# Two layers of four parallel mixers: half of the pool and conv denses moved ahead of the attention, five filler matmuls a step

## The chip, the cores and the metric

The kernel runs on one core of one Trainium2 chip. The metric is the device time of one execution in microseconds (us), here the median of three runs. TensorE (PE in the profile) does matmuls, VectorE (DVE) and ScalarE (ACT) the elementwise work, GpSimd (POOL) a few small operations and some DMAs, and SyncE (SP) issues most DMAs. Each engine takes its own instructions in the order in which the compiler left them and waits on semaphores for the others.

## The reference: what is computed

Two layers of a decoder trunk over 512 tokens of width 1024, all in float32:

```
h = rmsnorm(x, norm_g);  proj = h @ w_in           # split into the inputs of everything below
o_nsa  = nsa_mixer(...)    # compressed + selected + window attention, 4 heads of 64
o_pool = pool_mixer(...)   # causal means over 2, 4, 8, 16 tokens, then a 64x64 mix per group
o_conv = conv_mixer(...)   # b * (3-tap causal convolution of c * x)
o_fox  = fox_mixer(...)    # attention with forgetting gates, 4 heads of 64
branch_i = (o_i * silu(gates_i)) @ w_branch[i]     # 256 -> 1024
acc = sum_i sigmoid(merge_i) * branch_i            # merge_i: 4 x 1024 columns of proj
x = x + acc @ w_out                                # a final rmsnorm after the second layer
```

## The kernel before

Activations lie transposed: 128 features on the partitions, 512 tokens along the free dimension. Every float32 operand is split into a high part, rounded to the matmul's input format, and a low part, the rest (`split`, lines 69 to 76: ScalarE copies the high part, VectorE subtracts), and a product is three matmuls: high by high, high by low, low by high. A *dense* (lines 288 to 310) makes 128 output features for all tokens: 8 blocks of the 1024 inputs times 3 products, 24 matmuls of 512 columns into one of three PSUM banks `ps_d`. Its weights come by one 512 KB DMA into `wr`, and are split into `wh` and `wl`, two buffers each. Its result is taken over by a generator (`evac`) that is pumped one step for every second matmul, so that its VectorE and ScalarE steps fall under the next dense.

A layer runs in this order. The inputs of the compressed keys, of the selection and window keys and of the queries, then the values (`v_group`). Then eight gate denses, with the compressor's small products between them. Then the attention: 12 units, two for each of four NSA heads and one for each of four forgetting heads. A unit has four score products (`S`, lines 643 to 667: two matmuls into `ps_s`, a fused add and minimum on VectorE, the exponential with its sum on ScalarE, a reciprocal and a normalisation on VectorE), three groups of transposes (`T`, lines 673 to 681, 3 + 4 + 3 blocks into `ps_pt`, which are then split into `ptx`), and three groups of four matmuls with the values (`PV`, lines 683 to 703, into `ps_o`). After a head's last PV, `head_out` adds the two halves, multiplies by the gate and splits the result into `y`.

A loop over 57 steps (lines 1200 to 1216) lays the units out, one score product a step, the transposes from four steps later, the PV from seven. After each step it takes `FILL` matmuls from a chain of denses, the *filler* (lines 1170 to 1183): 4 denses for the forgetting heads, 4 for the first half of pool and convolution, 4 for the second half, 6 merge logits, 18 x 24 = 432 matmuls in all, of which 48 are taken before the loop. That is only the order in which the program is written. A scheduler puts each engine's instructions in an order of its own by what it takes to be ready, so that filler and merge denses can stand earlier than they are written.

After the attention come the branch products (`branches`, lines 821 to 844, 24 matmuls for each of four blocks of output features), the first of which are scheduled among the last attention steps; the rest of the merge logits; a second half of the merge with seven products in place of eight (`merge`); and the output projection. Its last block also gives the sum of squares for the next norm: `add_square` (line 238) squares a block of 128 features on ScalarE and adds it on VectorE to the blocks before it; `sum_squares` (line 229) then sums over the partitions with four one-column matmuls by a vector of ones. It does so once for the first seven blocks, when the seventh is added, and once for the eighth.

At the start, `ng` (norm gains, 128 x 24) is loaded on GpSimd's queue (line 1054). Each block of x is multiplied by it as it is split (`x_parts`). 16 idle matmuls on ones (line 1073) run before the first dense.

Of the kernel before, what the change touches and what calls it, by code (L numbers as in the profile page):

```python
# [16 lines left out]
T = 512  # L17
# [4 lines left out]
MERGE0 = 52  # L22
FILL = 7
ACT_NORM = ()
# [20 lines left out]
def trunk_kernel(ctx: ExitStack, tc: tile.TileContext, xT, w_all, par_all, const, gains, rope, outT):  # L45
# [47 lines left out]
    class Stream:  # L93
# [60 lines left out]
        def load(self, slot="wr"):  # L154
            i = self.loaded
            self.loaded += 1
            c = self.cols(i)
            self.slots.pop(next(n for n, x in enumerate(self.slots) if x is slot))
            if slot == "wr":
                t = sb([128, 1024], "wr", 3)  # L160
            elif slot == "rope":
                t = sb([128, 2, T], "rope", 1).rearrange("p a b -> p (a b)")
            else:
                t = slot
            l, j = self.order[i]
            if i == 0:
                for n in range(2):
                    nc.scalar.dma_start(t[:, n * 512:n * 512 + 512], w_all[l, j, :, n * 512:n * 512 + 512])
            else:
                nc.sync.dma_start(t[:, :c], w_all[l, j, :, :c])  # L170
            self.raw[i] = t, slot
# [65 lines left out]

    def add_square(src, m, bias=0.0, sq=None):
        n = src.shape[-1]
        sq = (temp() if sq is None else sq)[:, :n]  # L240
        ACT.activation(sq, src, AF.Square, bias=bias)
        if m in (0, 7):
            state["sq"] = sq
        else:
# [4 lines left out]
            else:  # L249
                DVE.tensor_tensor(state["sq"], state["sq"], sq, ALU.add)  # L250
            if m == 6:
                sum_squares(n, True, False)

    def stats(n=T, keep=False):
        sum_squares(n, False, True)
        p = state["ssq"]
# [796 lines left out]

    nc.gpsimd.dma_start(ng, gains)
    xr = []
# [16 lines left out]
    idle = psum("s", 2)  # L1072
    for n in range(16):
        PE.matmul(idle[:, 128:T], tri_ones[:, 128:256], tri_ones[:, 128:T], start=n == 0, stop=n == 15)

# [18 lines left out]
    for l in range(L):  # L1094
# [43 lines left out]
        def ev_gate(i, f):  # L1138
# [7 lines left out]
            return g  # L1146

        ch = None
        for n, (i, f) in enumerate(GATES):
# [5 lines left out]
            if n == 3:  # L1155
                drain()
                ch = itertools.chain(cmp_k(), cmp_v())
        drain()
        run(ch)
# [10 lines left out]
        def filler():  # L1170
            for f in range(2):
                yield from dense(rhs, ev_fq)
                yield from dense(rhs, ev_fk)
            yield from dense(rhs, ev_pool(0))
            yield from dense(rhs, ev_conv("x", 0))
            yield from with_mix(dense(rhs, ev_conv("c", 0)))
            yield from dense(rhs, ev_conv("b", 0))
            yield from dense(rhs, ev_pool(1))
# [3 lines left out]
            for m, i in LOGITS[:4 + AHEAD]:  # L1182
                yield from dense(rhs, ev_merge(m, i))

        def with_mix(d):
            for n, _ in enumerate(d):
                if n == 3:
                    mx = pool_mix()
                    next(mx)
                    bg.append(mx)  # L1190
                yield

# [56 lines left out]
        else:  # L1249
            xn = []  # L1250

            def ev_last(m, c):
                def g(acc):
# [3 lines left out]
                    DVE.tensor_tensor(x, acc[:, :c.stop - c.start], x, ALU.add)  # L1257
                    add_square(x, m)
                    if m == 1:
# [29 lines left out]
    for half in range(2):  # L1289
# [3 lines left out]
        drain()  # L1293
        _, rb = stats(T // 2, keep=True)
        x = xn[KT - 1][:, c]
# [56 lines left out]
def _layout(np, a):  # L1352
# [8 lines left out]
    for l in range(L):  # L1361
# [12 lines left out]
        for n, (i, h) in enumerate(GATES):  # L1374
            tiles.append(feat(run(2448 + 256 * i + 128 * h)))
            if n < 4:
                tiles.append(hid(n // 2, n % 2))
        for h in range(2):
            tiles += [feat(run(1676 + 128 * h)), feat(run(1932 + 128 * h))]
        for h in range(2):  # L1380
            tiles += [feat(run(s + 128 * h)) for s in (652, 908, 1420, 1164)]
        pairs = lambda m: [m[256 * j:256 * j + 256].reshape(2, 128, 512).transpose(1, 0, 2).reshape(128, 1024)
# [52 lines left out]
```

## Time and profile before

| | us |
|---|---|
| median of three runs | 954.16 (953.74 to 955.42) |
| the profiled execution | 953.55 |
| its span, first to last instruction | 951.0 |
| PE busy | 936.2 (98%) |
| VectorE busy | 714.0 (75%) |
| ScalarE busy | 520.0 (55%) |
| mean granted TensorE clock | 0.997 of full speed |

Busy time is the sum over stages with different limits, so the share of a stage says more than that of the span. A matmul's reported length is longer than the distance to the next one, as matmuls overlap: the pace is read from a run of them. A chain of waits follows the work that ended last backwards, at each step to what released it.

### The profile page before, as it was taken

The page shows a single profiled execution, that of the slowest core. Times are in us where ns is not written, and L with a number is a line of the kernel's source. Part 1 is how long each engine was busy: PE and PEld are TensorE (multiplying, and loading weights), DVE is VectorE, ACT ScalarE, POOL GpSimd, SP SyncE. Part 2 cuts the span into 40 slices and gives each one's busy share as a digit, 9 for nine tenths or more (in the row PEclk, how much of TensorE's full clock was granted, in tenths as well). Part 3 has the DMA queues.
Part 4 walks back from the last instruction along what each step waited for, and adds up shares of the span by engine and source line. Part 5 has one row for each costly group of instructions (what it writes and reads, how often), then busy time and mean ns, then how long its engine had stood idle before and what let it go on. Part 6 is the DMA issues. An engine that isn't in the chain of part 4 may idle for free.

```text
span 951.0 us, 12852 instructions
## 1 busy us (share of the span) xinstructions
PE 936.2 (98%) x4696; PEld 795.4 (84%) x4696; DVE 714.0 (75%) x1392; ACT 520.0 (55%) x906; POOL 31.1 (3%) x45
## 2 busy tenths in 40 slices
PE   9999999999999999999999999999999999999996
PEld 7988888888878888887889888888888788888796
DVE  6694689986787977776668548999677878686765
ACT  7295475575545554544426636656665455546273
POOL 0000000000000000000100000000000000010002
PEclk9999999999999999999999999999999999999998
DMA  7253222222236667643515421221322557686353
GB/s 268 80 175 113 74 83 68 78 89 89 67 122 173 171 207 213 177 155 134 189 63 170 135 89 67 89 67 45 111 67 79 177 159 201 200 210 194 112 168 121
DMA packets 39614, 124.73 MB, mean 131 GB/s; under 512 B 4464, under 2 KB 6528, under 8 KB 39552
## 3 DMA queue, kind: packets, MB, share of 16 engines
q1 hardware_dynamic: 35712, 112.38, 36.0%
q0 software_dynamic: 2976, 10.50, 5.5%
q10 hardware_dynamic: 864, 1.05, 0.3%
q8 instruction: 36, 0.59, 0.3%
q14 instruction: 26, 0.21, 0.1%
HBM read 119.72 MB, written 4.19 MB: 130 GB/s over the span
## 4 chain that ended last, share of the span: by engine, by line
PE 95%; DVE 2%; ACT 1%; DMA 1%; issue 1%; POOL 0%; DVEq 0%; SPq 0%; ACTq 0%; POOLq 0%
PE ps_d L303 56%; PE ps_d L988 9%; PE ps_s L988 5%; PE ps_o L698 3%; PE ps_pt L676 3%; PE ps_pt L988 2%; PE ps_pt L1026 2%; PE ps_s L554 2%; PE ps_pt L554 2%; PE ps_s L832 2%; PE ps_s L653 2%; PE ps_s L652 1%; PE ps_pt L832 1%; PE ps_o L1026 1%; PE ps_d L1026 1%; PE ps_o L415 1%
## 5 line engine op out<-in xcount | busy, mean ns | idle before, releaser
L303 PE MATMUL ps_d<-xh,wh 128*128 128x512 f32 x632 | 248.9, 394 | 1.9 <-ACT wh L72 1.9
L303 PE MATMUL ps_d<-xl,wh 128*128 128x512 f32 x632 | 248.6, 394 | 0.5 <-DVE xl L76 0.5
L72 ACT ACTIVATE wh<-wr 128x1024 fp32r<-128x1024 f32 (+2 forms) x134 | 139.0, 1038 | 153.9 <-PE ps_d L303 70.1
L73 DVE TENSOR_TENSOR wl<-wr,wh 128x1024 fp32r<-128x1024 f32 (+2 forms) x134 | 160.3, 1199 | 52.5 <-ACT wh L72 50.8
L303 PE MATMUL ps_d<-xh,wl 128*128 128x512 f32 x632 | 174.0, 392 | 0.0
L303 PEld LDWEIGHTS ps_d<-xh,wh 128*128 128x128 f32 x632 | 118.9, 188 | 25.7 <-ACT wh L72 3.0
L303 PEld LDWEIGHTS ps_d<-xl,wh 128*128 128x128 f32 x632 | 118.8, 188 | 24.0 <-DVE xl L76 1.5
L303 PEld LDWEIGHTS ps_d<-xh,wl 128*128 128x128 f32 x632 | 117.5, 188 | 23.1
L657 ACT ACTIVATE p<-p,nm 128x128 f32<-128x128 f32 (+1 forms) x96 | 53.3, 556 | 35.1 <-DVE nm L655 34.8
L324 DVE TENSOR_TENSOR t<-ps_d,rstd 128x512 f32<-128x512 f32 x74 | 50.7, 685 | 26.7 <-PE ps_d L303 26.3
L655 DVE CUSTOM_DVE_ANT_0 p<-ps_s,cst 128x128 f32<-128x128 f32 (+1 forms) x96 | 45.6, 484 | 13.0 <-PE ps_s L653 6.8
L72 ACT ACTIVATE ptx<-ps_pt 128x384 fp32r<-128x384 f32 (+1 forms) x72 | 36.9, 521 | 23.1 <-PE ps_o L698 14.3
L698 PE MATMUL ps_o<-ptx,V 128*128 128x256 f32 (+1 forms) x288 | 48.8, 282 | 0.6 <-DVE ptx L73 0.6
L698 PEld LDWEIGHTS ps_o<-ptx,V 128*128 128x128 f32 x288 | 42.4, 190 | 3.6 <-DVE ptx L73 0.8
L73 DVE TENSOR_TENSOR ptx<-ps_pt,ptx 128x384 fp32r<-128x384 f32 (+1 forms) x72 | 42.0, 592 | 2.1 <-ACT ptx L72 2.0
L676 PE MATMUL ps_pt<-cst,p 128*128 128x128 f32 x240 | 40.1, 276 | 0.0
L303 PE MATMUL ps_d<-y,wh 128*128 128x256 f32 (+1 forms) x176 | 38.0, 336 | 0.9 <-ACT y L75 0.9
L303 PE MATMUL ps_d<-st,wh 128*128 128x256 f32 (+1 forms) x176 | 33.5, 332 | 0.0
L73 DVE TENSOR_TENSOR wl<-V,wh 128x1024 fp32r<-128x1024 f32 x18 | 22.0, 1222 | 13.1 <-ACT wh L72 13.1
L303 PEld LDWEIGHTS ps_d<-y,wh 128*128 128x128 f32 x176 | 27.9, 190 | 4.2 <-ACT y L75 1.4
L72 ACT ACTIVATE wh<-V 128x1024 fp32r<-128x1024 f32 x18 | 19.1, 1062 | 21.9 <-PE ps_s L832 6.5
L676 PEld LDWEIGHTS ps_pt<-cst,p 128*128 128x128 f32 x240 | 28.1, 140 | 3.3
(343 smaller groups left out, 1736.4 us busy)
## 6 DMA issues: line engine op xcount, KB each, us to landing
wr<-in_w_all_dram SPq DMA_DIRECT2D x143, 512.0 KB, 3.3
V<-in_w_all_dram SPq DMA_DIRECT2D x26, 512.0 KB, 3.5
rope<-in_w_all_dram SPq DMA_DIRECT2D x12, 512.0 KB, 4.6
t<-in_xT_dram SPq DMA_DIRECT2D x16, 256.0 KB, 4.6
V<-in_w_all_dram POOLq DMA_DIRECT2D x8, 512.0 KB, 8.2
wr<-in_w_all_dram SPq DMA_DIRECT2D x8, 400.0 KB, 3.1
wr<-in_w_all_dram POOLq DMA_DIRECT2D x6, 512.0 KB, 6.8
ptc<-in_xT_dram SPq DMA_DIRECT2D x8, 256.0 KB, 3.1
```

The lines of the kernel that those rows point to most:

```text
L72: ACT.activation(hi, src, AF.Copy)
L73: DVE.tensor_tensor(lo, src, f32(hi), ALU.subtract)
L303: PE.matmul(acc[:, :width], w, r[k][:, tok], start=(n == 0), stop=(n == 23))
L324: DVE.tensor_tensor(t, acc, state["rb"], ALU.mult)
L554: PE.matmul(accs[tt][:, 0:400], x[:, tt * 128:tt * 128 + 128], w, start=(k == 0 and a == 0), stop=(kp == 3 and kk == 1 and a == 2))
L655: DVE.tensor_tensor_reduce(out=P[:, :n], in0=s[:, :n], in1=bias, scale=1.0, scalar=3e38, op0=ALU.add, op1=ALU.min, accum_out=nm)
L657: ACT.activation(P[:, :n], P[:, :n], AF.Exp, bias=nm, scale=-1.0, accum_out=sm)
L676: PE.transpose(p[:, c:c + 128], self.P[qt][:, kb * 128:kb * 128 + 128], ident)
L698: PE.matmul(dst, V[:, kb, self.vset, :], part[:, src], start=(self.fresh and self.cmp is None and b == 0 and kb == 0 and j == 0), stop=(se ...
L832: PE.matmul(p, w[:, c], r, start=(n == 0), stop=(n == 5))
L988: PE.matmul(bank[tt], x, w[:, d], start=(opens and k == 0 and n == 0), stop=(name in ("P2", "P3", "P4") and k == 3 and n == 2), skip_group ...
L1026: PE.matmul(p, x[:, c], w[:, d], start=(n == 0), stop=(n == 5))
```

## The change

Three things change. First, the first half of pool and convolution (`first_half`: four denses and the mixing product between them) is written after the last gate dense, ahead of the attention, instead of inside the filler; `FILL` goes from 7 to 5; and the host lays the weight tiles out in the new order. Second, the sum of squares adds all eight blocks first and has one set of one-column matmuls; only the second half of the final norm keeps two sets (`two`). Third, `ng` is loaded on ScalarE's queue between the two halves of the first weight tile, and 14 idle matmuls stand for 16. The weight loads, the matmuls of the denses and the attention's own operations are the same in number and shape.

```diff
-FILL = 7
+FILL = 5
@@ Stream.load, for the first tile
                 for n in range(2):
                     nc.scalar.dma_start(t[:, n * 512:n * 512 + 512], w_all[l, j, :, n * 512:n * 512 + 512])
+                    if n == 0:
+                        nc.scalar.dma_start(ng, gains)
@@
-    def add_square(src, m, bias=0.0, sq=None):
+    def add_square(src, m, bias=0.0, sq=None, two=False):
...
-        if m in (0, 7):
+        if m == 0 or (m == 7 and two):
             state["sq"] = sq
...
-            if m == 6:
+            if m == 6 and two:
                 sum_squares(n, True, False)
 
-    def stats(n=T, keep=False):
-        sum_squares(n, False, True)
+    def stats(n=T, keep=False, two=False):
+        sum_squares(n, not two, True)
@@
-    nc.gpsimd.dma_start(ng, gains)
...
-    for n in range(16):
+    for n in range(14):
@@
+        def first_half():
+
+            yield from dense(rhs, ev_pool(0))
+            yield from dense(rhs, ev_conv("x", 0))
+            yield from with_mix(dense(rhs, ev_conv("c", 0)))
+            yield from dense(rhs, ev_conv("b", 0))
+
         ch = None
         for n, (i, f) in enumerate(GATES):
...
                 ch = itertools.chain(cmp_k(), cmp_v())
+        run_with(first_half(), ch, 3)
         drain()
         run(ch)
@@ filler
-            yield from dense(rhs, ev_pool(0))
-            yield from dense(rhs, ev_conv("x", 0))
-            yield from with_mix(dense(rhs, ev_conv("c", 0)))
-            yield from dense(rhs, ev_conv("b", 0))
             yield from dense(rhs, ev_pool(1))
@@ the last projection and the final norm
-                    add_square(x, m)
+                    add_square(x, m, two=c.start > 0)
...
-        _, rb = stats(T // 2, keep=True)
+        _, rb = stats(T // 2, keep=True, two=half == 1)
```

What this does to the order of the engines is shown at three places. In the changed kernel the lines from 166 on are two or more higher: L652 to L667 are L654 to L669, L832 is L834.

PE in layer 0, where the last unit's last score product stands. `ps_s<-st` is a score, `ps_pt<-cst,p` a transpose, `ps_o<-ptx,V` a PV, `ps_s<-y,wh` a branch product, `ps_d` a dense. Before:

```order
L676 MATMUL ps_pt<-cst,p 128x128 x7
L652 MATMUL ps_s<-st 128x512
L653 MATMUL ps_s<-st 128x512
L832 MATMUL ps_s<-y,wh 128x512 x2
L832 MATMUL ps_s<-y,wl 128x512
L832 MATMUL ps_s<-y,wh 128x512 x2
L832 MATMUL ps_s<-y,wl 128x512
L303 MATMUL ps_d<-xh,wh 128x512
L303 MATMUL ps_d<-xl,wh 128x512
```

After it, in the changed kernel:

```order
L654 MATMUL ps_s<-st 128x384
L655 MATMUL ps_s<-st 128x384
L700 MATMUL ps_o<-ptx,V 128x256
L700 MATMUL ps_o<-ptx,V 128x128 x2
L678 MATMUL ps_pt<-cst,p 128x128
L654 MATMUL ps_s<-st 128x512
L655 MATMUL ps_s<-st 128x512
L834 MATMUL ps_s<-y,wh 128x512 x2
L834 MATMUL ps_s<-y,wl 128x512
L834 MATMUL ps_s<-y,wh 128x512 x2
L834 MATMUL ps_s<-y,wl 128x512
L678 MATMUL ps_pt<-cst,p 128x128 x6
```

Before, a dense of 24 matmuls follows the branch block, 19 of them in a row. In the changed kernel the eleventh unit's transposes follow it, and from the first scores of the twelfth unit to the last PV no dense stands.

VectorE at the same place, from its reduction of that last score (`p,nm<-ps_s,cst`). `ptx<-ps_pt,ptx` splits transposes, `t<-t,ps_s` applies a merge gate to a branch product, `p<-p,sm` normalises, `o` and `y` belong to a head's output, `p<-ptc` prepares the merge. Before:

```order
L655 ISA p,nm<-ps_s,cst 128x512
L655 ISA nm 128x1
L877 TENSOR_TENSOR p<-ptc 128x256
L73 TENSOR_TENSOR ptx<-ps_pt,ptx 128x512
L837 SCALAR_TENSOR_TENSOR t<-t,ps_s 128x512
L706 TENSOR_TENSOR o<-o,y 128x512
L658 RECIPROCAL sm<-sm 128x1
L667 TENSOR_SCALAR p<-p,sm 128x512
```

In the changed kernel, from the merge gate that now stands ahead of it:

```order
L839 SCALAR_TENSOR_TENSOR t<-t,ps_s 128x512
L708 TENSOR_TENSOR o<-o,y 128x512
L657 ISA p,nm<-ps_s,cst 128x512
L657 ISA nm 128x1
L669 TENSOR_SCALAR p<-p,sm 128x384
L879 TENSOR_TENSOR p<-ptc 128x256
L73 TENSOR_TENSOR ptx<-ps_pt,ptx 128x512
L73 TENSOR_TENSOR ptx<-ps_pt,ptx 128x384
L713 TENSOR_TENSOR y<-o,y 128x512
```

The merge gate, which stood behind the split of 512 columns, four places after the reduction, now stands ahead of the reduction, and both splits of the eleventh unit stand behind it.

ScalarE at the start of the program, before:

```order
L168 DMA wr<-in_w_all_dram 128x512 x2
L1067 ACT_TABLE_LOAD
L1067 ACTIVATE nhalf<-nhalf 128x4
L72 ACTIVATE wh<-wr 128x512
L75 ACTIVATE xh<-t,ng 128x512 x2
L72 ACTIVATE wh<-wr 128x512
L75 ACTIVATE xh<-t,ng 128x512
```

and in the changed kernel:

```order
L168 DMA wr<-in_w_all_dram 128x512
L170 DMA ng<-in_gains_dram 128x24
L168 DMA wr<-in_w_all_dram 128x512
L1068 ACT_TABLE_LOAD
L1068 ACTIVATE nhalf<-nhalf 128x4
L72 ACTIVATE wh<-wr 128x512
L75 ACTIVATE xh<-t,ng 128x512 x3
L72 ACTIVATE wh<-wr 128x512
```

The load of `ng` stands between the two weight halves, and the third x part goes ahead of the second half's split.

## Rows read from the trace of the kernel before

**Rows 1.** The page's first part: busy us (share of the span) x instructions.

```profile
PE 936.2 (98%) x4696; PEld 795.4 (84%) x4696; DVE 714.0 (75%) x1392; ACT 520.0 (55%) x906; POOL 31.1 (3%) x45
```

**Rows 2.** Stages, gates and attention: length, PE, PEld, DVE, ACT, POOL busy, PEclk, DMA share, GB/s.

```profile
75.00:105.00 30.00, 30.00 (x144) 24.91 (x143) 13.88 (x30) 11.75 (x21) 0.00 (x0) 1.00 0.32 106
115.00:278.00 163.00, 162.38 (x876) 139.04 (x875) 135.85 (x342) 100.88 (x210) 2.12 (x4) 1.00 0.25 78
```

**Rows 3.** Waits of PE's weight loads, 225 to 290: us, times, longest us.

```profile
PEld ps_s L832 <- DVE y L711: 1.3, 1, 1.3
PEld ps_d L303 <- ACT wh L72: 1.3, 1, 1.3
```

**Rows 4.** Chain of waits, end of layer 0's attention: start us, us, what.

```profile
261.99 0.66 PE ps_pt L676 x6
262.65 0.23 PE ps_s L652
...
274.81 0.93 PE ps_o L698 x8
...
277.93 0.30 PE ps_o L698 x3
```

**Rows 5.** The same chain, behind the last PV.

```profile
278.63 4.53 DMA V<-in_w_all_dram
...
285.82 4.38 PE ps_d L303 x18
```

**Rows 6.** Chain of waits, two merge denses in a row.

```profile
313.32 10.88 PE ps_d L303 x48
```

**Rows 7.** VectorE's groups, 225 to 290: count | busy us, mean ns | idle before.

```profile
L73 DVE TENSOR_TENSOR wl<-wr,wh 128x1024 fp32r<-128x1024 f32 x8 | 9.7, 1222 | 3.5 <-ACT wh L72 2.3 <-ACT ptx L72 1.2
L73 DVE TENSOR_TENSOR ptx<-ps_pt,ptx 128x384 fp32r<-128x384 f32 x9 | 5.0, 553 | 1.3 <-ACT ptx L72 1.3
...
L73 DVE TENSOR_TENSOR ptx<-ps_pt,ptx 128x512 fp32r<-128x512 f32 x5 | 3.4, 679 | 0.5 <-ACT ptx L72 0.5
L722 DVE TENSOR_TENSOR o<-ps_o,o 64x512 f32<-64x512 f32 x5 | 3.4, 678 | 0.1
L655 DVE CUSTOM_DVE_ANT_0 p<-ps_s,cst 128x512 f32<-128x512 f32 x4 | 2.8, 689 | 1.3 <-PE ps_pt L676 1.3
...
L658 DVE RECIPROCAL sm<-sm 128x1 f32<-128x1 f32 x15 | 2.4, 159 | 1.9 <-ACT p L657 1.9
...
L667 DVE TENSOR_SCALAR p<-p,sm 128x512 f32<-128x512 f32 x4 | 2.0, 488 | 0.1
...
L655 DVE DVE_READ_ACCUMULATOR2_ANT nm<- 128x1 f32 x15 | 1.2, 83 | 0.0
...
L655 DVE CUSTOM_DVE_ANT_0 p<-ps_s,cst 128x128 f32<-128x128 f32 x3 | 0.9, 284 | 0.0
L877 DVE TENSOR_TENSOR p<-ptc 128x256 f32<-128x256 f32 x2 | 0.8, 422 | 0.0
```

**Rows 8.** Timeline in the attention: start us, us, instruction [idle before <-releaser].

```profile
245.39 0.68 DVE L324 TENSOR_TENSOR t<-ps_d,rstd 128x512 f32<-128x512 f32 x1
...
245.99 0.55 DVE L73 TENSOR_TENSOR ptx<-ps_pt,ptx 128x384 fp32r<-128x384 f32 x1
...
246.59 0.56 PE L698 MATMUL ps_o<-ptx,V 128*128 128x256 f32 x3 [0.57 <-DVE ptx L73]
```

**Rows 9.** Timeline at layer 1's start: a set of column sums, and the matmul behind it.

```profile
476.41 0.95 PE L235 MATMUL ps_o<-onesf,p 128*128 128x1 f32 x8
...
477.22 0.49 PE L303 MATMUL ps_d<-xl,wh 128*128 128x512 f32 x1
```

**Rows 10.** Chain of waits, the program's start.

```profile
1.27 4.71 DMA ng<-in_gains_dram
```

**Rows 11.** Timeline of the same start.

```profile
1.90 5.49 PE L1074 MATMUL ps_s<-tri_ones 128*128 128x384 f32 x16 [1.90 <-DVE tri_ones L1070]
...
6.00 1.33 ACT L75 ACTIVATE xh<-t,ng 128x512 fp32r<-128x512 f32 x2 [0.81 <-DMA ng<-in_gains_dram]
```

More of the change, by code (lines that the diff above doesn't have):

```diff
@@ L1072, in trunk_kernel @@
     idle = psum("s", 2)
-    for n in range(16):
-        PE.matmul(idle[:, 128:T], tri_ones[:, 128:256], tri_ones[:, 128:T], start=n == 0, stop=n == 15)
+    for n in range(14):
+        PE.matmul(idle[:, 128:T], tri_ones[:, 128:256], tri_ones[:, 128:T], start=n == 0, stop=n == 13)
     def x_parts(k, src, g):
@@ L1146, in ev_gate, with with_mix @@
             return g
+        def with_mix(d):
+            for n, _ in enumerate(d):
+                if n == 3:
+                    mx = pool_mix()
+                    next(mx)
+                    bg.append(mx)
+                yield
+        def first_half():
[3 more added lines that the diff above has]
+            yield from dense(rhs, ev_conv("b", 0))
         ch = None
@@ L1183, in filler @@
                 yield from dense(rhs, ev_merge(m, i))
[L1185 to L1191, printed above, removed]
         fill = filler()
@@ L1377, in _layout @@
                 tiles.append(hid(n // 2, n % 2))
+        tiles += [feat(run(s)) for s in (652, 908, 1420, 1164)]
         for h in range(2):
             tiles += [feat(run(1676 + 128 * h)), feat(run(1932 + 128 * h))]
-        for h in range(2):
-            tiles += [feat(run(s + 128 * h)) for s in (652, 908, 1420, 1164)]
+        tiles += [feat(run(s + 128)) for s in (652, 908, 1420, 1164)]
         pairs = lambda m: [m[256 * j:256 * j + 256].reshape(2, 128, 512).transpose(1, 0, 2).reshape(128, 1024)
```

## The prediction

> **What bounds the kernel now.** I read the page's first part, the table of stages, PE's waits, then the chain of waits through the end of layer 0's attention. PE is busy for 98% of the span [rows 1], so time comes only from matmuls that go, or from places where PE stands still. In the gate stage VectorE is busy for 13.88 of 30 us; in the attention for 135.85 of 163, 83% [rows 2]. PE's longest waits lie at the attention's end: 1.3 us for the last y, 1.3 us for the next weights [rows 3]. There the chain goes from the score matmul of the last unit (262.65) through a dense block, the branch products and the last PV (277.93 + 0.30) [rows 4]. Behind it come two things that the change leaves alone: the V-buffer loads, released by the last PV, and the first dense of the next group, late by its weights [rows 5].
>
> PE's pace, for all sums below: a 512-column matmul 10.88/48 = 0.227 us [rows 6], a transpose 0.66/6 = 0.11, a PV matmul 0.93/8 = 0.116, a 512-column score matmul 0.23 [rows 4].
>
> **The change part by part.** Times are those of the profiled execution: 953.55 us, of which 951.0 is span. The median of the runs shown is 954.16, 0.6 above it.
>
> *Moved dense work.* Four denses and three mixing matmuls a layer (99 x 0.227 = 22.5 us of PE) go from the attention to the end of the gate stage. PE's own work is unchanged: at seven a step, 57 steps asked for 399 matmuls of 384 left; at five for 285 of 288. VectorE's part moves along: four weight halves and four scalings, 4 x (1.22 + 0.68) = 7.6 us, and about 14 passes of pool and convolution at 0.68, 9.5 us [rows 7]. In the gate stage these 17 us lie beside 22.5 us of dense work on an engine that was 46% busy [rows 2]: cost 0; were that cover gone, each evacuation would hold PE by its own 0.68. In the attention VectorE keeps 135.9 - 17 = 119 us in 163 - 22.5 = 140.5, 85% for 83%. So I expect the attention's middle unchanged: 0, bounded by 2.5 us a layer either way, four or five waits of the size that the last of [rows 8] shows (0.57). The host stores the weight tiles in the new order, so SP issues the same loads of the same size; only `par` goes ahead of one weight load.
>
> *The end of the attention*, the term that decides. Per step PE now has two dense matmuls fewer with which to wait for VectorE. The compiled order shows where that ends: before, 19 dense matmuls followed the last unit's final score matmul and its first branch block; now no dense matmul stands between the first scores of the twelfth unit and the last PV. I count from the 512-column score matmul of the eleventh unit to the last PV. PE has 24 branch and 1 dense matmul (5.7 us), 20 transposes (2.2), 36 PV (4.2), and scores of 3584 columns (1.6): 13.7 us. VectorE has 38 instructions between its reduction of that score and the last transpose split [rows 7]: reductions 0.69 + 0.69 + 0.28, and 0.42 and 0.55 for the two widths between: 2.6; their reads 0.4; five reciprocals 0.8; five normalisations from 0.49 down, 2.0; a weight half 1.2; five splits of 384 and two of 512 columns, 4.1; two head sums 1.4; four more of 512 columns 2.7; four of 256 at 0.42, 1.7. Sum 16.9. Instructions in a row start 0.60 apart where one reports 0.68 [rows 8], 0.08 less, 33 times: 16.9 - 2.6 = 14.3. So VectorE, not PE, is the longer.
>
> Lower bound, VectorE never waiting: the score is there at 0.65; the last split but one ends 0.65 + 14.3 - 0.5 = 14.5; PE then has four PV, six branch matmuls and four PV, 2.3: 16.8, against 13.7, a wait of 3.1. Upper bound, walking the three queues in order. Unit 10's last PV wait for a split that stands behind a weight half, which waits for ScalarE's half and so for the last dense: 1.4 us. Unit 11's second PV wait for a split that stands six places behind a merge-gate product, and this needs the branch block that PE has just finished: 2.7 us. Unit 12's wait 0.7. Together 4.8. [Rows 8] show the mechanism: the split for a PV came after a scaling that had nothing to do with it, and PE stood 0.57. Before, the 15.58 us from 262.65 to 278.23 hold 15.3 us of matmuls (a score pair 0.46, 24 branch and 24 dense 10.9, 10 transposes 1.1, 24 PV 2.8 [rows 4]): a wait of 0.3, or 0.6 with the 0.2 to 0.3 that such sums miss. So the change adds 2.6 to 4.4 us a layer; I take 3.3, toward the middle, since queues as blocked as in [rows 8] are what the row shows. The two layers have the same order here: +6.6. Behind the last PV both orders hold 24 branch matmuls, the same head sum and the weights of [rows 5]: 0.
>
> *Sums of squares.* Adding the eighth square on VectorE saves one set of column sums at three of four places. One set keeps the next matmul away for 477.22 - 476.41 = 0.81 us in a layer [rows 9], and half of that at the end, where it covers half the tokens: 2 x 0.81 + 0.4 = 2.0. Three additions come instead (0.68, 0.68, 0.42 by the widths in [rows 7]); in PE's order dense matmuls still stand between the last square and the remaining set, and hide them; uncovered they would cost 1.8. Taken: -2.0.
>
> *Start.* `ng` leaves POOL's queue for ScalarE's, between the halves of the first weight tile. It landed 4.71 us after issue, and the first x part waited 0.81 us for it with ScalarE free [rows 10, 11]. Gained: up to 0.8. Then x tiles still coming in, or ScalarE's own chain, are next; as the second weight half is pushed back by one small transfer, it could lose 0.3. Taken: -0.6. The two idle matmuls (2 x 0.34 [rows 11]) end earlier than PE is wanted: in the same 0.6.
>
> By the Trainium skill's page "DMA: Bandwidth & Descriptors" (Specifications) a queue like ScalarE's has its first byte some 0.4 us sooner than POOL's, but rows under 512 bytes, and those of `ng` have 96, miss line rate; as an estimate, the first alone would make this term -0.4, the second 0. No run here shows either yet.
>
> Sum: 953.55 - 2.0 - 0.6 + 6.6 = 957.55; I say **957.5**.
>
> **Rivals.** 0.2%, 1.9 us, is about what a measurement can tell from no change: faster is below 952.25, slower above 956.07.
>
> *Not slower: VectorE's relief pays.* The pool and convolution work that stood among attention steps blocked splits as in [rows 8]; without the first half of it, waits of that size (0.57 to 0.8) go. Four fewer a layer give 2 x 3.2 = 6.4: 957.5 - 6.4 = 951.1. It decides if more than 3.3 a layer comes back, or the end waits less than 1.3. For it: the middle of the attention has the densest VectorE. Against: the share stays at 85%, and PE has less to run meanwhile.
>
> *The change does little.* The order is made by the scheduler, not by the step count; if VectorE runs ahead at the end so that only 1.3 a layer stay: 953.55 - 2.6 + 2.6 = 953.6. For it: before, the same scheduler's order cost almost no wait. Against: the reduction of the counted score cannot run ahead, and 14.3 us follow it.
>
> *The whole attention starves.* Five matmuls cover less than the chain from score to transpose everywhere: 0.57 at each of four middle units a layer, 4.6 more: 962. Against: 85% is no more than before.
>
> *The clock falls in the longer waits.* The granted clock is 1.00 in all stages of [rows 2], with no wait above 1.3 us; at the start 16 matmuls of 384 columns took 5.49 us [rows 11], 0.34 each, the lower level of 1.2 GHz. A 2.7 us wait could bring that back for about as long, half of it lost: 2.8 a layer, 963. The Trainium skill's "TensorE: Matmul & The Clock Gate" (Part 1: The HAM clock gate) says that idleness throttles the array to 1.2 GHz; by that rule this rival would come true if a wait grew long enough, and the trace has no case inside the kernel.
>
> **How the numbers follow.** Forecast 0.45, with its own range 955 to 960 (2.6 to 4.4 a layer, the start, part of the middle); relief 0.28; little 0.15; starving 0.10; clock 0.02. The range leaves out the lower part of relief (0.06), some of the forecast (0.02) and the last two above (0.11): 950.0 to 960.5. Faster: relief 0.25, little 0.03. Same: relief 0.03, little 0.12, forecast 0.08. Slower: 0.37 + 0.12.
>
> **What would show it.** Right: PE waits for ptx splits of 1 to 3 us in the last 15 us of each attention; VectorE near 95% busy there; one set of column sums per layer, with no wait before it; the first xh starting by 5.5. Wrong: waits below 1.3 us there, or a middle of the attention that runs over 2 us a layer faster or slower than its matmuls say.

## The result, and the profile after

The changed kernel takes 959.70 us (median of five runs, 957.54 to 961.01) against 953.74 of the kernel before beside it: 1.0057 of its time, with a 95% interval of 1.0045 to 1.0070, so 5.4 us more (4.3 to 6.7; the ratio is taken over all runs, the two medians alone differ by 6.0). Forecast were 957.5, 3.3 more than the median shown before and 4.0 more than the profiled execution that the sum starts from, in a range that holds the result.

The profiled execution took 961.01, the longest of the five; its span is 959.2. The page's first part answers to [rows 1]; the two stages, the same 30 us of gates and the attention from its first score to its last PV, to [rows 2]. In the second fence the columns are those of [rows 2].

```profile
PE 938.1 (98%) x4674; PEld 793.8 (83%) x4674; DVE 716.6 (75%) x1395; ACT 519.8 (54%) x906; POOL 29.8 (3%) x44
```

```profile
75.00:105.00 30.00, 30.00 (x142) 24.84 (x142) 14.48 (x30) 11.15 (x19) 0.00 (x0) 1.00 0.32 106
137.00:279.00 142.00, 139.98 (x773) 120.08 (x772) 118.93 (x315) 92.69 (x200) 2.07 (x4) 1.00 0.23 75
```

VectorE's part of the attention is 118.93 of 142 us, 84%, where 119 of 140.5 were worked out. What PE loses by waiting hides in such shares: 98% stands for PE in both kernels. It shows in the waits of PE's weight loads at the end of layer 0's attention, 240 to 295 us, which answer to [rows 3]:

```profile
PEld ps_o L700 <- DVE ptx L73: 1.3, 2, 1.0
PEld ps_s L834 <- DVE y L713: 1.3, 1, 1.3
PEld ps_s L834 <- ACT y L711: 1.2, 1, 1.2
PEld ps_pt L834 <- DVE t L839: 0.9, 1, 0.9
PEld ps_d L305 <- ACT wh L72: 0.9, 1, 0.9
PEld ps_o L700 <- DVE o L724: 0.4, 1, 0.4
PEld ps_o L700 <- ACT ptx L72: 0.3, 1, 0.3
```

The second and the fifth were there before, and so, smaller, were one wait for a split (0.8) and one for a merge gate (0.2). The five others are new or have grown: three of them name VectorE, and a fourth, y of L711, is ScalarE's copy of a head's output that VectorE had just multiplied by its gate (L708). The chain of waits through the same place shows it better than any sum. In [rows 4] this chain went from one piece of PE's work to the next, with one stay outside PE, the split of a weight tile:

```profile
271.25 1.06 ACT wh L72
...
272.33 1.24 DVE wl L73
```

After the change (start us, us, what):

```profile
261.43 0.68 DVE o L724
...
266.72 0.46 DVE ptx L73
267.18 0.39 DVE p L669
267.64 0.19 DVE p L669
267.86 0.70 DVE o L724
268.58 0.35 DVE p L669
269.00 0.58 DVE t L839
269.59 0.60 DVE o L708
270.19 0.60 DVE p L657
...
274.52 0.46 DVE ptx L73
```

From 261.43 to 274.98 all its longer pieces but two of issue (0.09 and 0.38 us) are VectorE's, 26 of them: by this chain it is VectorE's work that decides when PE can go on. VectorE is busy for 15.47 of the 16.98 us that follow from the counted score on. The stretch that the prediction counted, from the eleventh unit's last score to the last PV, runs from 262.09 to 279.07 in layer 0 and from 730.35 to 747.31 in layer 1: 16.98 and 16.96 us. Worked out were 16.8 with VectorE as the bound and 18.5 with the queues walked, so the result lies near the first.

To compare kernels whose orders differ, I take from every trace the start of each matmul and subtract what the same matmuls take in an undisturbed run (0.227 us for 512 columns, 0.12 for 256, 0.06 to 0.09 for 128). What is left over in a stretch is called its waits here. How large it is hangs on the paces taken, so only differences between kernels are used. Between the two profiled executions the span grew from 951.0 to 959.2 us (the time by 7.46, as what lies outside the span differs too). These 8.2 us came together thus:

| part | forecast | in the traces |
|---|---|---|
| start of the program | -0.6 | -0.1 |
| column sums | -2.0 | -2.2 of matmuls, +0.9 of a new stall |
| attention up to the eleventh unit's last score | 0 (2.5 a layer either way) | -0.8 and -0.1 |
| from there to the last PV | +3.3 a layer | +2.9 and +2.8 |
| the 60 matmuls behind the last PV | 0 | +0.4 and +3.6 |
| the rest, by difference | 0 | +0.8 |

Of the 3.6 in layer 1 nearly half is the clock. PE's rows there, and two stretches with their granted clock (the column behind POOL's):

```profile
752.40 0.63 PE L834 MATMUL ps_s<-y,wh 128*128 128x512 f32 x2
753.91 0.50 PE L834 MATMUL ps_s<-y,wh 128*128 128x512 f32 x1 [0.88 <-DVE y L713]
...
756.68 0.60 PE L305 MATMUL ps_d<-xh,wh 128*128 128x512 f32 x1 [1.57 <-ACT wh L72]
757.08 0.63 PE L305 MATMUL ps_d<-xl,wh 128*128 128x512 f32 x1
757.51 0.63 PE L305 MATMUL ps_d<-xh,wh 128*128 128x512 f32 x1
...
760.43 0.39 PE L305 MATMUL ps_d<-xl,wh 128*128 128x512 f32 x1
760.66 0.39 PE L305 MATMUL ps_d<-xh,wh 128*128 128x512 f32 x1
```

```profile
752.00:757.00 5.00, 2.54 (x10) 1.47 (x9) 4.34 (x8) 2.49 (x4) 0.00 (x0) 0.99 0.39 156
757.00:767.00 10.00, 10.00 (x38) 8.09 (x37) 7.85 (x13) 3.48 (x8) 0.94 (x1) 0.83 0.76 188
```

In the 5 us before, PE was busy for 2.54. Then eight dense matmuls start 0.427 apart, the lower level of 1.2 GHz, before the distance is 0.23 again: 8 x 0.2 = 1.6 us. Of the remaining 2.0 most are waits for a merge gate (0.67, new), for y (1.05 for 0.4) and for the weights (1.75 for 1.22). In layer 0 of the same execution the clock stayed at 1.00, and the excess there is 0.4.

### The profile page after: what moved, and what is told of

Same layout as the page of the kernel before. It is cut to its first block, busy times and chain, and to the rows that moved or that the text cites. A ratio compares the mean times of both kernels' runs of the same rounds, so it can differ in the third digit from the quotient of the medians.

```text
span 959.2 us, 12822 instructions
## 1 busy us (share of the span) xinstructions
PE 938.1 (98%) x4674; PEld 793.8 (83%) x4674; DVE 716.6 (75%) x1395; ACT 519.8 (54%) x906; POOL 29.8 (3%) x44
## 4 chain that ended last, share of the span: by engine, by line
PE 93%; DVE 4%; DMA 2%; ACT 1%; issue 0%; SPq 0%; POOL 0%; DVEq 0%; ACTq 0%
PE ps_d L305 55%; PE ps_d L990 9%; PE ps_s L990 5%; PE ps_o L700 3%; PE ps_pt L990 2%; PE ps_pt L1028 2%; PE ps_pt L678 2%; PE ps_s L556 2%; PE ps_pt L556 2%; PE ps_s L655 1%; PE ps_s L654 1%; PE ps_pt L834 1%; PE ps_s L834 1%; PE ps_o L1028 1%; PE ps_d L1028 1%; PE ps_o L417 1%
## 5 line engine op out<-in xcount | busy, mean ns | idle before, releaser
L654 PE MATMUL ps_s<-st 128*128 128x128 f32 (+1 forms) x96 | 31.0, 327 | 0.0
```

Source lines behind the costliest of these rows:

```text
L654: PE.matmul(s[:, :n], q[:, c], kh[:, :n], start=True, stop=False)
```

## The experiments

Every kernel was timed in turn with the kernel before on the same chip; the ratios are to those runs, whose medians were 953.74 for the changed kernel, 952.80 for the next four, 953.94 for the four after them and 953.81 for the last four. So kernels of different groups are compared by their ratios. The last column gives the waits in the stretch from the eleventh unit's last score to the last PV, in layer 0 and layer 1, from one profiled execution each.

| kernel | median us | ratio (95%) | waits at the end |
|---|---|---|---|
| before | 953.74 | 1 | 1.4, 1.5 |
| changed | 959.70 | 1.0057 (1.0045 to 1.0070) | 4.3, 4.3 |
| small edits only | 953.14 | 0.9998 (0.9990 to 1.0007) | 1.4, 1.5 |
| reorder only | 960.24 | 1.0079 (1.0065 to 1.0093) | 4.3, 4.3 |
| changed, four a step | 960.90 | 1.0086 (1.0072 to 1.0100) | 4.5, 6.5 |
| changed, seven a step | 966.66 | 1.0150 (1.0133 to 1.0167) | 6.9, 6.4 |
| two denses moved | 951.74 | 0.9981 (0.9972 to 0.9990) | 1.4, 1.6 |
| changed, no merge preparation | 960.79 | 1.0071 (1.0056 to 1.0087) | 5.8, 4.3 |
| column sums only | 953.48 | 0.9992 (0.9983 to 1.0000) | 1.5, 1.5 |
| gains' load only | 954.95 | 1.0011 (1.0000 to 1.0023) | 1.4, 1.5 |
| before, four logits in the filler | 957.97 | 1.0043 (1.0028 to 1.0059) | 4.4, 4.4 |
| changed, narrow gates | 956.18 | 1.0023 (1.0012 to 1.0033) | 3.9, 3.9 |
| three denses moved | 958.92 | 1.0045 (1.0031 to 1.0059) | 2.5, 6.3 |
| two moved, seven logits | 955.38 | 1.0017 (0.9997 to 1.0036) | 1.1, 1.0 |

**The two halves of the change.** The changed kernel with the reorder undone:

```diff
-FILL = 5
+FILL = 7
-        run_with(first_half(), ch, 3)
@@ filler
+            yield from first_half()
             yield from dense(rhs, ev_pool(1))
```

> The changed kernel with the reorder undone: the first half of pool and convolution back in the filler, seven matmuls a step; the single set of column sums and the new place of the norm gains' load stay. Theory A (the reorder alone costs, at the end of each attention; the small edits gain about 2): 951.5 to 952.7, 1.0 to 2.2 below before, and 7 to 8 below the changed kernel; PE's waits over 0.3 us at the attention's end as in before. Rival B (the reorder is neutral and the small edits cost, by the 0.9 us stall at 493 us behind the single set of column sums and the like): 956 or more, within 3 of the changed kernel.

And the reorder without the small edits (two sets of column sums, `ng` on GpSimd's queue, 16 idle matmuls):

> The kernel before with the reorder alone: first half of pool and convolution ahead of the attention, five a step; two sets of column sums and the gains' load on GpSimd's queue as before. Theory A: 960 to 962, 6 to 8 above before, waits of 4.3 us from the eleventh unit's last scores to the last PV in each layer as in the changed kernel. Rival B: 953 to 955, within 1.5 of before.

The reorder alone costs 7.5 us (6.2 to 8.9), with the waits at the attention's end of the changed kernel. The small edits alone change nothing that can be told from zero (1.0 less to 0.7 more). Theory A holds for the reorder; its 1.0 to 2.2 for the small edits does not, and rival B falls.

**How many filler matmuls a step.** `FILL = 4` and `FILL = 7` in the changed kernel:

> The changed kernel with four filler matmuls a step for five: the same instructions, but a block of 24 dense matmuls now stands ahead of the twelfth unit's first scores, where five to seven steps earlier it stood in the changed kernel. Theory A (what costs is that no dense matmul is left for the chain at the end, while VectorE has a queue of work): VectorE can work its queue off during that block, so the wait from there to the last PV falls from 4.3 to 1.5 to 3 a layer; the middle loses at most 1 of it; 956 to 958.5. Rival C (the attention as a whole is bound by VectorE, and PE's waits only move): 959 to 961, the excess of the whole attention within 0.7 a layer of the changed kernel's 9.5.

> The changed kernel with seven filler matmuls a step: the dense matmuls keep their places, but 12 of the first branch matmuls of each layer go from among the last unit's steps to behind the last PV. Theory A: the end of the attention loses 2.7 us of cover in each layer, its wait grows from 4.3 to 6 to 7, but the 1.0 wait for the last y behind the last PV is covered by the twelve: net +0.5 to +1.7 a layer, 960.5 to 963. Rival D (the branch blocks between the splits hold the splits up more than they cover, since a merge gate stands ahead of a split): the wait falls, 955 to 958.

At four a step theory A failed in what it said of VectorE. The dense block of 24, which in the compiled order stands just behind the first of the twelfth unit's four score products, did not let VectorE work its queue off to any use: the waits behind it are 4.5 and 6.5, and the time is that of the reorder. The waits of PE's weight loads in layer 0's last steps (256 to 280 us) name another thing that stands in the same queue, the half of a head's sum that frees the output bank:

```profile
PEld ps_o L700 <- DVE o L724: 1.5, 1, 1.5
PEld ps_s L654 <- DVE nm L657: 0.8, 1, 0.8
```

Rival C's numbers came true in layer 0 (9.4 of waits in the whole attention for 9.5), not in layer 1 (12.2). At seven a step the waits grow to 6.9 and 6.4, as theory A had it, and rival D falls. But the time is 966.7, above both: the twelve branch matmuls behind the last PV covered nothing there; in layer 1 a wait of 3.8 us stands among them, and in 760 to 764 us the granted clock is 0.57. It is 0.57 in 272 to 276 us too, so part of layer 0's 6.9 is clock, not waiting: there PE had just stood for 2.5 us, until 272.68, for a split that frees a bank for transposes. The mean granted clock of this kernel's four runs is 0.991 to 0.996, where the changed kernel has 0.994 to 0.998; as an estimate, the 0.003 between their means are 3 us of the 966.7. Fewer matmuls among the last steps is worse; a block ahead of them doesn't help. What is left to ask is whether dense matmuls among them do.

**Two denses moved for four.** Pool and the x part of convolution go ahead; the c and b parts and the mix stay in the filler:

```diff
         def first_half():
 
             yield from dense(rhs, ev_pool(0))
             yield from dense(rhs, ev_conv("x", 0))
+
+        def rest_of_half():
+
             yield from with_mix(dense(rhs, ev_conv("c", 0)))
             yield from dense(rhs, ev_conv("b", 0))
@@ filler
+            yield from rest_of_half()
             yield from dense(rhs, ev_pool(1))
```

> The changed kernel with two of the four dense products moved ahead of the attention (pool and the x part of convolution); the c and b parts with the mix stand in the filler again, six matmuls a step. 24 + 24 dense matmuls a layer move for 99 with the mix. The compiled order of the attention's end is again that of the kernel before: 19 dense matmuls behind the last scores, 5 more before the last PV. Theory A (the loss is the attention's end without dense matmuls, nothing else): no waits over 0.8 us from the last scores to the last PV, time 951 to 953.5, within 0.15% of the small edits alone, while the amount of work moved is half of that of the changed kernel. Rival E (the loss grows with the work moved, since the attention has less for PE to run meanwhile): half of the reorder's 7.5, 956 to 957.5.

They do. No wait over 0.8 stands between the last scores and the last PV, and the time is 951.74, the fastest of all here, 1.8 us (1.0 to 2.7) below before. Theory A holds, but for its 0.15% to the small edits alone, which is 0.17%; rival E falls. This version beats both kernels. What it gains was not traced: its small edits give nothing by themselves, and its interval touches theirs (at 0.9990). The chain of waits through its attention's end is PE's again, as in [rows 4], in layer 0 with the 19 dense matmuls behind the first branch block (layer 1 has 15 and then 10):

```profile
261.23 0.23 PE ps_s L655
261.46 1.39 PE ps_s L834 x6
262.85 4.31 PE ps_d L305 x19
267.15 0.58 PE ps_o L700 x5
267.73 0.70 PE ps_d L305 x3
268.43 0.33 PE ps_pt L678 x3
```

**A bare end without any move.** The kernel before, with two merge logits fewer in the filler:

```diff
-AHEAD = 2
+AHEAD = 0
```

> The kernel before with four merge logits in the filler for six (two denses a layer, 48 matmuls, go behind the attention, to the merge); nothing is moved ahead of the attention, no small edit. The attention then has 424 dense matmuls a layer, as many as the version with two denses moved ahead, but its compiled order has none of them from the twelfth unit's first scores to the last PV. Theory A (a bare end is what costs, whatever left it bare): PE's waits there 4 to 6 a layer, 957.5 to 961. Rival J (the work that was moved ahead of the attention is what costs, by what it does to the gate stage or the weight loads): within 1 of before.

Its attention has 424 dense matmuls a layer, as many as the kernel with two denses moved, and nothing went ahead of it. Its last 24 stand behind the first of the twelfth unit's four score products in layer 0, not ahead of them all as expected, and from the unit's last score to the last PV there is none. Still it costs 4.1 us (2.7 to 5.6), with waits of 4.4 in each layer where before had 1.4 and 1.5, and the same releasers as in the kernel with four a step (weight loads, 246 to 270 us):

```profile
PEld ps_o L698 <- DVE o L722: 1.5, 1, 1.5
PEld ps_s L652 <- DVE nm L655: 0.5, 1, 0.5
```

So it is the place of the dense matmuls and not their amount, and not what the moved work does in the gate stage. Rival J falls. The median lies within what theory A gave, near its lower end.

**Three denses moved.** The same with the c part and the mix ahead too:

> The changed kernel with three of the four denses moved ahead, the b part of convolution back in the filler, six a step. One dense block (24) more in the attention than in the changed kernel, one less than with two moved; in the compiled order three dense matmuls stand just ahead of the last scores, and none behind them. Theory A (a bare end): PE waits 3 to 4.5 a layer there, 957 to 960. Rival E (the loss goes with the work moved): by the two points known, none at two denses and 7 at four, about 955.

958.92, in theory A's range and out of rival E's 955: between two and three denses the loss comes with the order, and not in proportion. Its waits, 2.5 and 6.3, are more uneven than the 3 to 4.5 expected, so most of the loss is layer 1's; the two layers have different orders there.

**VectorE's queue.** Two kernels took work off it. The first leaves out the four elementwise steps that prepare the merge (so the merge's values are not computed):

```diff
-            DVE.tensor_tensor(tmp[:, 0], xa[0][:, lo_], xa[0][:, hi_], ALU.subtract)
+            POOL.memset(tmp[:, 0], 0.5)
...
-            DVE.tensor_tensor(s1[:, c], xa[1][:, hi_], xa[0][:, hi_], ALU.subtract)
+            POOL.memset(s1[:, c], 0.5)
```

> The changed kernel without the four subtractions on VectorE that prepare the merge (L879 to L887); GpSimd fills their outputs with a constant, so the merge's result is left out. Five of them, 256 wide, 0.42 us each, stand among the last 38 VectorE instructions of each attention, four of them ahead of a split that PE waits for. Theory A (VectorE's queue is what PE waits for at the end): the wait from the eleventh unit's last scores to the last PV falls from 4.3 to 2.4 to 3.2 a layer, and the time by 2 to 4 against the changed kernel, to 955.5 to 957.7. Rival F (PE waits there for the chain through ScalarE and the semaphores, VectorE's queue is not the bound): the wait stays above 3.9 a layer and the time within 1 of the changed kernel.

Nothing was gained: 960.79, and by its numbers rival F. But the scheduler gave this kernel another order. The twelfth unit's first three transposes now stand ahead of the second branch block (and the 5.8 in layer 0 hold a fall of the granted clock, 0.91 in 262 to 281 us). Its six runs also had a lower mean granted clock than the changed kernel's five, 0.994 for 0.997, by estimate 2.7 us of its time, so the time alone does not settle it; the waits, which did not fall, speak against theory A's 2.4 to 3.2. The row where PE waits longest in layer 1's stretch names the split again, one of a pair that stands behind a merge gate, a reduction and the multiplication of a head's output by its gate (L708):

```profile
738.72 0.68 DVE L839 SCALAR_TENSOR_TENSOR t<-t,ps_s 128x512 f32<-128x512 f32 x1
...
739.32 0.69 DVE L657 CUSTOM_DVE_ANT_0 p<-ps_s,cst 128x512 f32<-128x512 f32 x1
...
739.93 0.69 DVE L708 TENSOR_TENSOR o<-o,y 128x512 f32<-128x512 f32 x1
...
740.53 1.15 DVE L73 TENSOR_TENSOR ptx<-ps_pt,ptx 128x512 fp32r<-128x512 f32 x2
...
741.37 0.52 PE L678 MATMUL ps_pt<-cst,p 128*128 128x128 f32 x3 [1.79 <-DVE ptx L73]
```

The experiment tells less than it was meant to. The second kernel keeps the order: the merge gate works on a quarter of its columns (the rest of the merge is left unscaled).

```diff
-            DVE.scalar_tensor_tensor(sg, sg, 1.0, p, op0=ALU.add, op1=ALU.mult)
+            DVE.scalar_tensor_tensor(sg[:, :128], sg[:, :128], 1.0, p[:, :128], op0=ALU.add, op1=ALU.mult)
```

> The changed kernel with the merge gate in the branch products (L839) applied to 128 of 512 columns, so that each takes about 0.25 us on VectorE for 0.67; the merge's result is left out for the rest. The compiled order of the attention's end stays as it is but for one pair of splits at its end. Two of these gates stand among the last VectorE instructions ahead of the last PV, each ahead of a split or of the y that PE waits for. Theory A (PE waits there for what stands ahead in VectorE's queue): the time from the eleventh unit's last scores to the last PV falls by 0.4 to 0.9 a layer from 17.0, and the 0.67 us wait for a gate behind the last PV goes; 957 to 959. Rival F (the chain is bound by ScalarE and semaphores): the stretch stays within 0.2 of 17.0.

One place in layer 0, in the changed kernel and then with narrow gates: the merge gate, the multiplication of a head's output by its own gate behind it (L708), and PE's wait for the y that is made from this output.

```profile
268.92 0.67 DVE L839 SCALAR_TENSOR_TENSOR t<-t,ps_s 128x512 f32<-128x512 f32 x1
269.50 0.68 DVE L708 TENSOR_TENSOR o<-o,y 128x512 f32<-128x512 f32 x1
...
270.90 0.96 PE L834 MATMUL ps_s<-y,wh 128*128 128x512 f32 x3 [0.96 <-ACT y L711]
```

```profile
268.75 0.27 DVE L839 SCALAR_TENSOR_TENSOR t<-t,ps_s 128x128 f32<-128x128 f32 x1
268.93 0.69 DVE L708 TENSOR_TENSOR o<-o,y 128x512 f32<-128x512 f32 x1
...
270.37 0.96 PE L834 MATMUL ps_s<-y,wh 128*128 128x512 f32 x3 [0.59 <-ACT y L711]
```

The merge gate is 0.40 shorter, and PE, which does not use its result, waits 0.37 less. The stretch goes from 16.98 to 16.61, 0.37 less and a little under the 0.4 to 0.9 expected; the second gate in it gave nothing. Behind the last PV the new wait for a gate is gone (waits of 2.1 and 2.2 in those 60 matmuls for 2.9 and 5.6), and the median is 956.18, below the 957 expected: between the two profiled executions more came back behind the last PV than in the stretch. Rival F's stretch within 0.2 of 17.0 did not come, so a wait behind other work in VectorE's queue is shown in the one place; how much of the 4.3 the queue makes in all, and how much the chain through ScalarE, stays open.

**The small edits apart.**

> The kernel before with the single set of column sums alone. PE has 20 column-sum matmuls fewer, about 2.2 us with what they hold up. Theory G (0.9 of it goes again into a stall ahead of the hidden layer's first products in layer 1, where the changed order puts these straight behind a dense whose weight buffer they need): 0.9 to 1.6 below before, 951.2 to 952. Rival H (the order changes elsewhere too and all of it is lost): 952.5 to 953.3. By the prediction's own term: 2.0 below, 950.8.

> The kernel before with the norm gains' load on ScalarE's queue and 14 idle matmuls alone. Theory G (the first dense matmul starts 0.9 to 1.0 us earlier, but the x parts and the second weight half that follow hold the next ones, so that the tenth starts 0.1 to 0.2 earlier): within 0.4 of before. Rival I (the second weight half comes so late that the start loses): 0.5 to 1 above before. By the prediction's own term: 0.6 below.

The single set of sums gives 0.8 us (0 to 1.6), just under theory G's 0.9 to 1.6 and clear of the term's 2.0; rival H is not shut out. Its profiled execution is 1.3 below that of before (by the span 0.5, 950.5 for 951.0) and shows both sides of G: 20 matmuls fewer, and this stall in layer 1 (the row is that of the changed kernel, which has the same):

```profile
493.60 0.87 ACT L72 ACTIVATE wh<-wr 128x800 fp32r<-128x800 f32 x1 [0.80 <-PE ps_d L305]
...
494.52 0.65 PE L556 MATMUL ps_s<-wh,xh 128*128 128x400 f32 x2 [0.72 <-ACT wh L72]
```

Before, another dense of 24 stood between this weight split and the hidden layer's products. The gains' load came out at 1.0 above before (0 to 2.2), with runs from 952.44 to 958.38; the profiled one is 952.44, and in it the eleventh dense matmul started 0.7 earlier than before and the fiftieth 0.6, more than G's 0.1 to 0.2. Neither G nor I is settled by the time, which goes with the granted clock: 0.992 in the longest run, 0.997 in the shortest. The trace of the changed kernel shows G's mechanism: `ng` landed 4.2 us after issue for 4.71 [rows 10], the first x part started at 5.45 for 6.00 [rows 11], the first dense matmul at 6.31 for 7.19, but the eleventh at 10.61 for 10.78.

**More dense work at the end still.** The kernel with two denses moved and `AHEAD = 3`:

> The version with two denses moved ahead, and seven merge logits in the filler for six, so that a dense of 24 stands between the last unit's transposes and its last PV too. Theory A: there is little left to cover before the last PV (no wait over 0.8 there), so at most 0.6 a layer can come; the waits for the last y and the next weights behind the last PV remain: 950.3 to 952. Rival K (the branch products come later by that dense, and with them the merge's transfers): 952.5 to 955.

The waits before the last PV fall to 1.1 and 1.0, as theory A has it. The time does not: 955.38, with runs from 951.90 to 961.71, with an interval that holds no change, just above K's 952.5 to 955. In its profiled execution (952.56) the wait for the next weights in layer 0 is 1.6 us, and the granted clock 0.91 in 280 to 299 us. Part of the spread is the clock: the longest run had a granted clock of 0.991 and the shortest 0.998, by estimate 0.007 of 955 us or 6.7 of the 9.8 between them. But 959.59 came at 0.996, so that is not all, and the rest was not found.

## Why the prediction was right, and where it was not

**The attention's end** is the step that decides, and it held. The stretch took 16.98 us, inside 16.8 to 18.5; it added 2.9 and 2.8 us a layer for the 3.3 forecast, inside 2.6 to 4.4. Of its signs, VectorE was busy for 91% of the stretch (near 95% expected), and the longest weight load that waited for a split waited 1.0 us, just inside 1 to 3. The step from the lower bound toward the middle, for blocked queues, was not borne out: the stretch came 0.2 above the lower bound. The walk behind the upper bound was off: its longest wait, placed at the eleventh unit's second PV (2.7 us), came as one of 1.23 at the branch block, which needs a y whose multiplication by the gate stands in the same queue. Also, the prediction counted the wait of before, 0.3 to 0.6, from the twelfth unit's score and that of the changed kernel from the eleventh's; over the same stretch, by the counting used here, before has 1.4 and the changed kernel 4.3. The experiments show the cause from both sides: a bare end costs without a move (the four-logit kernel), and a move costs nothing while the end has its dense matmuls (two moved).

**The attention's middle**, forecast at 0 with 2.5 a layer to either side, gave 0.8 and 0.1 back. The rival that VectorE's relief pays had this as its whole mechanism and needed 3.3 a layer. The rival that everything starves had 0.57 at each of four places; in layer 0 the middle's waits per us did not rise (5.24 in 125 us for 6.06 in 133), in layer 1 by nothing to speak of (5.25 in 125 for 5.39 in 132).

**Moved denses** were costed at 0 in the gate stage, and the kernel with two moved agrees: its stretch from the first dense matmul to the first score has 0.7 of waits more than before, all but 0.1 of it from starting 0.6 earlier on the same x tiles.

**Sums of squares**: forecast -2.0, that is the term that was mis-sized. The matmuls gave 2.2; 0.9 came back as a stall at a weight buffer, since the set that went had stood between denses whose order then changed too. **Start**: forecast -0.6, and -0.1 in the trace. The prediction had written that "x tiles still coming in, or ScalarE's own chain, are next", and they were: in the changed kernel the third x part waits 0.38 us for its x tile, and the seventh dense matmul (9.57) waits for a weight split of ScalarE's. By the Trainium skill's page "DMA: Bandwidth & Descriptors" (Specifications), the first byte on such a queue comes about 0.4 us sooner; the landing, 4.2 for 4.71, fits that, but no row here shows the first byte by itself. Without the reorder both together gave 0.2 for the 2.6 forecast. Beside it, the ratios 1.0079 and 1.0057 put them at 2.1, with intervals that overlap; whether they are worth more there stays open.

**Behind the last PV**, forecast at 0, since both orders hold the same work there. The work is the same, but VectorE comes to it late: the merge gates queue behind the splits, and PE waits 0.7 for one in each layer. This step failed, by 0.4 in layer 0 and, without the clock, by 2.0 in layer 1.

That the total came out near is in part luck. In the profiled execution the end and the middle of the attention came out 0.9 each below their terms, the two small edits took off 1.2 less than theirs, the matmuls behind the last PV took 4.0 more, and 0.8 is in no term: 8.2 us in all for the 4.0 of the sum.

**The clock** had a chance of 0.02 as a rival. It fell in one of the two layers of the profiled execution and took 1.6 us, but it is no mark of the change: in the kernel with the small edits alone it fell in layer 0 at the same place (284 to 288 us):

```profile
284.00:288.00 4.00, 3.43 (x9) 2.59 (x9) 4.00 (x6) 1.66 (x2) 0.00 (x0) 0.64 0.38 131
```

In the profiled executions of before, of the reorder alone and of the kernel with two moved it did not. The Trainium skill's page "TensorE: Matmul & The Clock Gate" (Part 1: The HAM clock gate) has idleness as the cause, and the traces agree in that both falls come with the waits for the last y and the next weights; waits much like them left the clock up in other kernels, as the last section shows. The rival's own mechanism, a fall after one wait of some 2.7 us among the attention's last steps, is seen in two other kernels: at seven a step (a wait of 2.5, layer 0) and without the merge preparation (2.3, layer 0). In the changed kernel no wait there was longer than 1.23.

## What to carry to other kernels

Filler has a place, not only an amount. Before moving independent matmuls away from a chain that goes back and forth between engines, look where the scheduler leaves the last of them: with the same 424 dense matmuls in the attention, the kernel whose last 24 stood among the closing steps lost nothing, and the one without lost 4 us. And move half before moving all: the loss came between two denses and three, most of it in one layer.

## What was not expected of the hardware

The granted clock fell without any single long wait. In the changed kernel PE stood for 0.67, 1.05 and 1.75 us between 750 and 757 us and ran eight matmuls at the lower level; in the kernel with the small edits alone a fall came with waits of 1.08 and 0.74 us. The kernel with the column sums alone stood for 0.4 and 1.46 us in layer 1 and kept 1.00. The kernel before stood for 1.05 and 0.98 in layer 0 and kept it too, and at seven a step PE stood for 2.5 us in layer 1's last steps without a fall there. So a wait behind the last PV can cost more than its own length, in some executions.
